# When the loads for the up-projection's sums are issued, and where the last group's second norm is worked out, in a one-core encoder layer on Trainium2

## The chip, the core and the metric

The kernel runs on one core of one Trainium2 chip, in one launch. The metric is device time in microseconds, from the start to the end of the execution. The core has TensorE (matmuls), VectorE, ScalarE and GpSimd, and SyncE, whose queue issues nearly all DMAs of this kernel, in order: a DMA that has to wait for something holds all later ones back. Each engine works through its own instructions in order, too.

## The reference

One layer of a streaming encoder, for 2048 prompt tokens and 64 sample tokens (2112 in all), in float32:

```python
mod = (c_act @ w_ada + b_ada)[:, None, :]
sh1, sc1, gt1, sh2, sc2, gt2 = jnp.split(mod, 6, -1)
h = rmsnorm(x, g1) * (1 + sc1) + sh1
proj = h @ w_in                                  # 1024 -> 512 + 4*512 + 8
u, q, k, v, o, gates = jnp.split(proj, cuts, -1)
pool_out, pool_buf_new = pool_mixer(u, pool_buf, start, w_pool, s_pool)
hs, C, n, m = mlstm_seq(q, k * HEAD_DIM ** -0.5, v, ig, lf, C, n, m)
...
mix = jnp.concatenate([pool_out, hs], -1) @ w_out
x = x + gt1 * mix
h2 = rmsnorm(x, g2) * (1 + sc2) + sh2            # the second norm
up = h2 @ w_up                                   # 1024 -> 2 * 2816
conv = b_conv + sum(w_conv[j] * upp[:, j:j + T] for j in range(CONV_W))
a, g = jnp.split(conv, 2, -1)
x = x + gt2 * ((jax.nn.silu(g) * a) @ w_down)
```

A final RMSNorm follows. The two things that the change touches are the second norm, whose factor for a token is one over the root of the mean of the squares of the token's 1024 values of x after the first half, and the up-projection's weights `w_up`.

## The kernel before, in words

All large matmuls are done in three passes of a high and a low part of each operand. Data lie with channels on partitions and tokens along the free dimension; a "row" below is 128 channels by the tokens of a group.

The **first half** (up to about 805 us of the span) goes over four groups of tokens, 512 each and 576 in the last, numbered 0 to 3. For each: the projection of v and the gates (`proj_v`, matmuls at L1091), q, k and o (`gemm`, L445), the mLSTM of each head (L1188 to L1302), the pooling mixer, and the out-projection with its residual (`outproj`), which writes the eight rows of x to the DRAM tensor `x2d` (L608). In the mLSTM of a head, VectorE copies the small gate tiles CL and GL out of PSUM and makes kw, the weighted keys; TensorE needs CL at L1201, GL at L1255 in the last group and kw at L1280. The names of the helpers stand at L237 for many of these operations.

Beside the matmuls run generators that are advanced a step at a time: `bg[0]` holds the gates and the mLSTM of the heads, `bg[1]` the norms of the next group, `bg[3]` the conditioning `ada` (VectorE steps `s<-raw,CA` and `acc<-raw,CA` at L195 and L197, whose `raw` tiles are loads of `w_ada`, L181), and `bg[4]`, from group 1 on, `up_sums`.

`up_sums` prepares the **second half**, which forms the up-projection from seven products of sums of rows and of weights instead of eight. It has 44 steps. A step loads a tile w of 128 x 1024 values of `w_up` with two DMAs (L824), makes four sums and differences of 128 x 256 in place on VectorE (L838, L839, L841, L842), and stores the tile to the DRAM tensor `wsum` (L847). There are four buffers of w, so a load into a buffer waits until the store that last read it has landed: the wait stands at the head of SyncE's queue. Three loads are issued ahead of the first step; at the end of step i the load for step i+3 is issued, and right behind it step i's own store. The sums and both kinds of DMA keep their program order among themselves; where they fall among the other instructions of VectorE and SyncE in groups 1 to 3 is decided by a scheduler that orders instructions ahead of time. From the start of the second half on, and in the first steps of group 0, TensorE, ScalarE, VectorE and GpSimd keep the written order.

The **second half** (about 805 to 2229 us) goes over three token groups of 704: up-projection (`Pair.products`, L1531, with ScalarE copies `s` and `u` at L1570 and L1579 and VectorE sums `ea` and `eg`), convolution and gate, down-projection (L1807). Its input rows hx are split into high and low parts at L738 and L745.

The **second norm** of groups 0 to 2 is worked out in the out-projection: `sq_acc` squares each finished row on ScalarE (L479, into a scratch tile) and adds it to `ssum` on VectorE (L480); then TensorE sums over the partitions and the result goes to the columns of RS2. For the last group (`o.last`) the squares and adds are the same, but the end is `stat2`: a generator on `bg[0]` that idles for twelve steps, into the first products of the second half, and then calls `rstd_cols` (TensorE, L489). The columns of RS2 of the last group are read when the input of the third token group of the second half is prepared.

Of the kernel before, what the change touches and what calls it, by code (L numbers as in the profile page):

```python
# [11 lines left out]
AF = mybir.ActivationFunctionType  # L12
ALU = mybir.AluOpType
# [5 lines left out]
KD = D // P  # L19
# [37 lines left out]
def tile_layer(ctx: ExitStack, tc: tile.TileContext, xT, vecs, cst, rst, w_mod, w_ada, w_qkou, w_v, w_pool,  # L57
               w_out, w_up, w_down, st_C, st_pool, yT, o_pool, o_C, o_m, o_conv):
    nc = tc.nc
# [34 lines left out]
    bg = ([], [], [], [], [])  # L94
# [149 lines left out]
    for g in range(NG):  # L244
        o = Grp()
# [329 lines left out]
            if k != 3:  # L575
                yield

    def stat2(o, ssum):
        out = RS2[:, 4 * o.g:4 * o.g + len(o.chunks)]
        for _ in range(12):  # L580
            yield
        rstd_cols([ssum], o, out)
        yield

    def outproj(o, mix, between):

        order = [4, 5, 6, 7, 3, 2, 1, 0]
        ssum = None if o.last else ssum_tile()
        now = Urgent(nc.vector)
        nx = [load_x(n, o) for n in (0, 1)]  # L590
        for rows in [(0, 1)] + [(n,) for n in range(2, KD)]:
            xs = nx
            Ws = [Row() for _ in rows]
            pss = [[mm_ps() for _ in o.blks] for _ in rows]
            if len(rows) == 1:
                gemm(pss[0], Ws[0], mix, o, order=order, ups=(4,))
            else:
                for W, ps in zip(Ws, pss):
                    gemm(ps, W, mix, o, ks=order[:6], order=order)
                quiet.clear()  # L600
                for W, ps in zip(Ws, pss):
                    gemm(ps, W, mix, o, ks=order[6:], order=order, late=1)
            nx = [load_x(rows[-1] + 1, o)] if rows[-1] + 1 < KD else []
            for n, x, ps in zip(rows, xs, pss):
                for (bi, pa, pb, a, b, s) in o.pieces:
                    now.scalar_tensor_tensor(out=x[:, a:b], in0=ps[bi][:, pa:pb], scalar=gt1(n, s), in1=x[:, a:b],
                                             op0=ALU.mult, op1=ALU.add)
                nc.sync.dma_start(out=x2d[n, :, o.t0:o.t0 + o.T], in_=x[:, :o.T])  # L608
            if rows[0] == 0:
                between()  # L610
                if o.last:
                    ssum = fscr("ssum")
            for n, x in zip(rows, xs):
                sq_acc(ssum, x[:, :o.T], o.T, n == 0)
        if o.last:
            bg[0].append(stat2(o, ssum))
        else:
            side.append(rstd_rows(ssum, o, RS2[:, 4 * o.g:4 * o.g + len(o.chunks)], []))

# [11 lines left out]
    def fscr(dt=F32):  # L631
        if dt in ("rb", "ssum"):
            return spare[0].tile([P, FT], F32, tag=dt, name=dt)
        return spare[0].tile([P, FT], dt, tag="fscr", name="fscr", bufs=6)
# [177 lines left out]
    if True:  # L812
# [6 lines left out]
        def up_sums():  # L819
# [12 lines left out]
            for i, (f, c) in enumerate(todo):  # L832
                w = nx.pop(0)
                yield
                yield

                a0, a1_, g0, g1 = (w[:, i, :] for i in range(4))
                pin(dve.tensor_tensor(out=g1, in0=g0, in1=g1, op=ALU.add))  # L838
                pin(dve.tensor_tensor(out=g0, in0=a0, in1=g0, op=ALU.subtract))  # L839
                yield  # L840
                pin(dve.tensor_tensor(out=a0, in0=g1, in1=a0, op=ALU.subtract))  # L841
                pin(dve.tensor_tensor(out=a1_, in0=a1_, in1=a0, op=ALU.subtract))  # L842
                yield

                if i + 3 < len(todo):
                    nx.append(load(*todo[i + 3]))
                pin(nc.sync.dma_start(out=wsum[f, :, :, c:c + 256], in_=w))  # L847

        def fold():
# [633 lines left out]
    todo = []  # L1483
# [475 lines left out]
```

## Time and profile before

| | |
|---|---|
| three runs | 2225.89, 2227.15, 2227.29 us (median 2227.15) |
| profiled execution | 2230.81 us |
| its span in the profile | 2229.0 us (1.81 us lie outside it) |
| mean granted TensorE clock | 0.996 |
| TensorE busy | 2208.9 us |
| VectorE, ScalarE, GpSimd busy | 1572.2, 1000.4, 192.5 us |
| DMA | 487.26 MB, mean 219 GB/s over the span |
| SyncE at L824, waiting for a wsum store | 100.4 us in 36 waits, longest 5.8 us |

The profile's lines name a line of the kernel, an engine and an operation, and `out<-in` by the names of the tiles, with buffer numbers left out: `w<-w_up` is a load of `up_sums`, `wsum<-w` its store. An arrow in square brackets gives the idle time of the engine ahead of the instruction, and what ended it. A wait on SyncE costs nothing by itself; it matters if a DMA behind it comes too late for an engine on which TensorE waits.

### The profile page before, as it was taken

What the parts mean: (1) busy time and instruction counts of PE and PEld (TensorE: products, weight loads), DVE (VectorE), ACT (ScalarE), POOL (GpSimd) and SP (SyncE); (2) the same over time, 40 slices, a digit from 0 to 9 for tenths busy, and PEclk for the clock granted to TensorE, in tenths of its full rate; (3) what the DMA queues carried; (4) which work ended last, traced back from release to release, by engine and by line L of the source; (5) the groups of instructions that cost most, each with busy time, mean ns of one, the idle gap of its engine ahead of it and who ended that gap; (6) DMA issues with size and microseconds to landing.
All of it is one profiled execution on the core that took longest, in us unless ns stands there. A gap on an engine that the chain in (4) does not pass through costs nothing.

```text
span 2229.0 us, 37990 instructions
## 1 busy us (share of the span) xinstructions
PE 2208.9 (99%) x13744; PEld 2102.7 (94%) x13744; DVE 1572.2 (71%) x2888; ACT 1000.4 (45%) x1981; POOL 192.5 (9%) x474
## 2 busy tenths in 40 slices
PE   8999999999999999999999999999999999999998
PEld 7888888888899999999999999999999999999998
DVE  5867668757955688687858587777766675757475
ACT  4644335234333455454536354545444343445254
POOL 0010000001000100010000210100001210101012
PEclk9999999999999999999999999999999999999999
DMA  9977997988879485747557775466458655353442
GB/s 350 330 251 228 300 305 254 306 286 266 296 253 299 148 269 164 243 163 270 179 176 243 263 263 176 156 213 198 143 160 290 196 167 167 111 171 116 145 148 81
DMA packets 284708, 487.26 MB, mean 219 GB/s; under 512 B 24640, under 2 KB 88512, under 8 KB 284520
## 3 DMA queue, kind: packets, MB, share of 16 engines
q1 hardware_dynamic: 275080, 462.52, 63.2%
q10 hardware_dynamic: 9440, 22.32, 2.6%
q8 instruction: 108, 1.77, 0.3%
q14 instruction: 80, 0.66, 0.1%
HBM read 378.68 MB, written 106.06 MB: 217 GB/s over the span
## 4 chain that ended last, share of the span: by engine, by line
PE 94%; DMA 3%; DVE 2%; issue 1%; SPq 0%; ACT 0%; POOL 0%; POOLq 0%; DVEq 0%; ACTq 0%
PE mm L1531 40%; PE mm L1807 23%; PE mm L445 23%; PE mm L1091 1%; DMA raw<-w_ada 1%; PE m L1280 1%; PE m L1300 1%; PE m L1302 1%; PE m L1265 1%; DMA wsum<-w 1%; PE mm L1028 1%; PE p L1028 1%; PE m L923 0%; PE m L1255 0%; DVE scr L237 0%
## 5 line engine op out<-in xcount | busy, mean ns | idle before, releaser
L1531 PE MATMUL mm<-hx,wt 128*128 128x352 f32 x5544 | 897.9, 323 | 1.9 <-ACT s L1570 1.3
L1531 PEld LDWEIGHTS mm<-hx,wt 128*128 128x128 f32 x5544 | 892.8, 188 | 2.6 <-ACT s L1570 1.6
L1807 PE MATMUL mm<-av,wt 128*128 128x352 f32 (+2 forms) x3168 | 514.5, 323 | 0.0
L1807 PEld LDWEIGHTS mm<-av,wt 128*128 128x128 f32 x3168 | 509.6, 188 | 1.2
L445 PE MATMUL mm<-hl,wt 128*128 128x512 f32 (+2 forms) x1920 | 389.7, 358 | 0.0
L379 ACT ACTIVATE wt<-raw 128x512 fp32r<-128x512 f32 (+3 forms) x518 | 286.2, 574 | 215.6 <-PE mm L445 77.6
L382 DVE TENSOR_TENSOR wt<-raw,wt 128x512 fp32r<-128x512 f32 (+3 forms) x518 | 324.4, 641 | 78.4 <-ACT wt L379 75.6
L445 PEld LDWEIGHTS mm<-hl,wt 128*128 128x128 f32 x1920 | 315.4, 189 | 52.5 <-issue 5.3
L1823 DVE SCALAR_TENSOR_TENSOR x<-mm,MOD,x 128x352 f32<-128x352 f32 (+4 forms) x224 | 106.5, 526 | 133.1 <-PE mm L1807 132.9
L445 PE MATMUL mm<-mx,wt 128*128 128x512 f32 (+1 forms) x960 | 185.3, 354 | 0.0
L445 PEld LDWEIGHTS mm<-mx,wt 128*128 128x128 f32 x960 | 159.1, 188 | 25.4
L1518 DVE SCALAR_TENSOR_TENSOR tg<-eg,V,tg 128x704 f32<-128x704 f32 (+1 forms) x132 | 125.7, 953 | 53.9 <-ACT tg L1513 51.6
L382 DVE TENSOR_TENSOR wt<-wt 128x512 fp32r<-128x512 f32 x176 | 121.7, 692 | 36.9 <-ACT wt L379 36.9
L1518 DVE SCALAR_TENSOR_TENSOR ta<-ea,V,ta 128x704 f32<-128x704 f32 (+1 forms) x132 | 125.7, 952 | 5.2 <-ACT ta L1513 2.6
L379 ACT ACTIVATE wt<-wt 128x512 fp32r<-128x512 f32 x176 | 108.3, 622 | 18.3 <-DMA wt<-wsum 14.6
L1579 ACT ACTIVATE u<-mm 128x352 f32<-128x352 f32 x66 | 30.7, 465 | 169.5 <-PE mm L1531 162.0
L1539 DVE TENSOR_TENSOR eg<-mm,u 128x352 f32<-128x352 f32 x154 | 70.2, 468 | 41.2 <-ACT u L1594 27.1
L1639 DVE TENSOR_TENSOR av<-tg,av 128x704 fp32r<-128x704 f32 (+1 forms) x88 | 60.6, 709 | 53.8 <-ACT av L1634 53.8
L1625 ACT ACTIVATE tg<-tg 128x704 f32<-128x704 f32 (+1 forms) x66 | 52.4, 794 | 78.5 <-DVE tg L1518 78.5
L1570 ACT ACTIVATE s<-mm 128x352 f32<-128x352 f32 x66 | 30.7, 465 | 111.4 <-PE mm L1531 106.9
L1091 PE MATMUL mm<-wt,hl 128*128 128x256 f32 (+1 forms) x576 | 70.7, 282 | 0.0
L1091 PEld LDWEIGHTS mm<-wt,hl 128*128 128x128 f32 x576 | 69.8, 188 | 0.9 <-issue 0.6
(293 smaller groups left out, 1954.3 us busy)
## 6 DMA issues: line engine op xcount, KB each, us to landing
raw<-w_up SPq DMA_DIRECT2D x198, 256.0 KB, 4.0
wt<-hl_kept SPq DMA_DIRECT2D x96, 512.0 KB, 6.0
wt<-wsum SPq DMA_DIRECT2D x176, 256.0 KB, 4.0
wt<-wsplit SPq DMA_DIRECT2D x88, 512.0 KB, 4.6
raw<-w_down SPq DMA_DIRECT2D x96, 256.0 KB, 3.0
w<-w_up SPq DMA_DIRECT2D x88, 256.0 KB, 4.0
wsum<-w SPq DMA_DIRECT2D x44, 512.0 KB, 5.1
wsplit<-wt SPq DMA_DIRECT2D x44, 512.0 KB, 3.3
```

Of the source, the lines that this page charges most:

```text
L379: act.activation(u.w[:, 0, :u.n], u.raw[:, :u.n], AF.Copy)
L382: dve.tensor_tensor(out=u.w[:, 1, :u.n], in0=u.raw[:, :u.n], in1=u.w[:, 0, :u.n].bitcast(F32), op=ALU.subtract)
L445: pe.matmul(ps[bi][:, :hi - lo], U[:, a, k % 4 * P:(k % 4 + 1) * P], mv[k][:, b, lo:hi], start=(at == 0 and pi == 0), stop=(k == order[-1] ...
L1028: pe.matmul(to[ti][:, :n], h[k][:, b, ti * P:(ti + 1) * P], w[:, a, k % 2 * n:(k % 2 + 1) * n], start=(hv == 1 and k == 0 and (a, b) == (0 ...
L1091: pe.matmul(ps[ti][:n, :cols], h[4 * kh + k4][:, b, lo:lo + n], U[:, a, k4 % 2 * cols:(k4 % 2 + 1) * cols], start=(kh == 0 and k4 == 0 and ...
L1518: dve.scalar_tensor_tensor(out=t[:, :E], in0=ext[:, j:j + E], scalar=wc(j, f), in1=t[:, :E], op0=ALU.mult, op1=ALU.add)
L1531: pe.matmul(ps[:, :FH], U[:, a, kc * P:(kc + 1) * P], Bo.at(nm, kc, b), start=(first and kc == 0 and pi == 0), stop=(kc == 3 and pi == 2), ...
L1539: dve.tensor_tensor(out=ext[:, d:d + b - a], in0=ps[:, a:b], in1=u[:, a:b], op=ALU.add)
L1625: act.activation(self.tg[:, :E], self.tg[:, :E], AF.Silu)
L1639: dve.tensor_tensor(out=self.d[:, 1, a:b], in0=self.tg[:, a + 2 * s:b + 2 * s], in1=self.d[:, 0, a:b].bitcast(F32), op=ALU.subtract)
L1807: pe.matmul(ps[i][:, :hi - lo], U[:, a, k % 4 * P:(k % 4 + 1) * P], av[k][:, b, lo:hi], start=(k == 0 and (a, b) == PASSES[0]), stop=(k == ...
L1823: dve.scalar_tensor_tensor(out=x3[n][:, a:b], in0=ps[i][:, a - lo:b - lo], scalar=gt2(n, s), in1=x3[n][:, a:b], op0=ALU.mult, op1=ALU.add)
```

## The change

In `up_sums` the load for a later step moves. Up to now it is issued at the end of step i, for step i+3, ahead of step i's store. Now it is issued in the middle of step i, ahead of the sums, for step i+2, and so behind the store of step i-1; steps 0, 42 and 43 issue none. There are still three loads ahead of the first step and four buffers.

In the out-projection of the last group, the squares and the adds are left out. `stat2` instead loads the eight rows of the group from `x2d` again (128 x 576 values, 288 KB each, SyncE), two ahead and then one per step, into scratch tiles of the second half; it squares them on ScalarE and adds them on VectorE, a step of the generator for each, and then calls `rstd_cols` as before. It runs during the first products of the second half.

```diff
-    def stat2(o, ssum):
-        out = RS2[:, 4 * o.g:4 * o.g + len(o.chunks)]
-        for _ in range(12):
-            yield
-        rstd_cols([ssum], o, out)
+    def stat2(o):
+
+        def load(k):
+            x = fscr()
+            nc.sync.dma_start(out=x[:, :o.T], in_=x2d[k, :, o.t0:o.t0 + o.T])
+            return x
+        nx = [load(0), load(1)]
+        ssum = fscr("ssum")
+        yield
+        for k in range(KD):
+            x = nx.pop(0)
+            yield
+            act.activation((x if k else ssum)[:, :o.T], x[:, :o.T], AF.Square)
+            yield
+            if k:
+                dve.tensor_tensor(out=ssum[:, :o.T], in0=ssum[:, :o.T], in1=x[:, :o.T], op=ALU.add)
+            if k + 2 < KD:
+                nx.append(load(k + 2))
+        yield
+        rstd_cols([ssum], o, RS2[:, 4 * o.g:4 * o.g + len(o.chunks)])
         yield
...
             if rows[0] == 0:
                 between()
-                if o.last:
-                    ssum = fscr("ssum")
             for n, x in zip(rows, xs):
-                sq_acc(ssum, x[:, :o.T], o.T, n == 0)
+                if not o.last:
+                    sq_acc(ssum, x[:, :o.T], o.T, n == 0)
         if o.last:
-            bg[0].append(stat2(o, ssum))
+            bg[0].append(stat2(o))
...
                 w = nx.pop(0)
                 yield
                 yield
+                if 0 < i < len(todo) - 2:
+                    nx.append(load(*todo[i + 2]))
 
                 a0, a1_, g0, g1 = (w[:, i, :] for i in range(4))
...
                 yield
-
-                if i + 3 < len(todo):
-                    nx.append(load(*todo[i + 3]))
                 pin(nc.sync.dma_start(out=wsum[f, :, :, c:c + 256], in_=w))
```

The line numbers of the kernel after the change are larger: by 15 in the lines from `outproj` on (L608 is L623), by 14 or 13 from `up_sums` on (L824 is L838, L847 is L860, L1280 is L1293, L1531 is L1544).

## The prediction

> **What bounds the kernel now.** I read the page's engine busy times and chain first, then the waits of TensorE, then the windows by stage, then the timeline around each wait that the change can reach.
>
> ```profile
> PE 2208.9 (99%) x13744; PEld 2102.7 (94%) x13744; DVE 1572.2 (71%) x2888; ACT 1000.4 (45%) x1981; POOL 192.5 (9%) x474
> PE 94%; DMA 3%; DVE 2%; issue 1%; SPq 0%; ACT 0%; POOL 0%; POOLq 0%; DVEq 0%; ACTq 0%
> ```
> ```profile
> PE m L1255 <- DVE GL L237: 2.0, 1, 2.0
> PE m L1280 <- DVE kw L237: 2.0, 1, 2.0
> PE mm L1531 <- ACT s L1570: 1.3, 1, 1.3
> PE mm L1531 <- DVE hx L745: 0.6, 1, 0.6
> ```
> ```profile
> 218.00:270.00 52.00, 50.04 (x324) 44.45 (x324) 33.45 (x67) 13.67 (x28) 1.01 (x1) 0.97 0.91 301
> 440.00:576.00 136.00, 136.00 (x678) 110.44 (x677) 96.60 (x217) 58.08 (x147) 10.51 (x16) 1.00 0.85 276
> 576.00:645.00 69.00, 67.00 (x501) 63.59 (x500) 49.38 (x102) 19.87 (x47) 1.11 (x1) 1.00 0.86 288
> 801.00:830.00 29.00, 27.15 (x175) 26.54 (x174) 22.24 (x46) 14.16 (x28) 2.90 (x6) 1.00 0.76 245
> ```
> TensorE is busy 99% of the span, and the change neither adds nor removes a matmul: it can only win back stalls or make new ones. VectorE (71%) and ScalarE (45%) are not the bound over a stage, so the work on them that moves costs only where TensorE waits behind it. In the windows (columns: length, busy TensorE, weight loads, VectorE, ScalarE, GpSimd, then granted clock, DMA share, GB/s) TensorE is idle 1.96, 2.00 and 1.85 us in the three stages where such waits stand, and not at all in 440 to 576. The reach of the change is therefore a few microseconds out of 2229, around 0.3%. I call the stalls A (266), B (642) and C (807 and 811).
>
> **Stall A, group 1.** The chain of waits, then the timeline:
>
> ```profile
> 252.82 3.92 DMA wsum<-w
> 256.75 0.55 SPq L824
> 258.30 0.56 SPq L847
> 258.92 5.12 DMA raw<-w_ada
> ```
> ```profile
> 264.13 0.75 DVE L197 SCALAR_TENSOR_TENSOR s<-raw,CA,s 128x512 f32<-128x512 f32 x1 [7.70 <-DMA raw<-w_ada]
> 265.54 0.69 DVE L237 TENSOR_TENSOR kw<-m,CL 128x512 f32<-128x512 f32 x1
> 266.38 1.82 PE L1280 MATMUL m<-va,kw 128*128 128x129 f32 x8 [1.96 <-DVE kw L237]
> 267.84 4.03 PE L445 MATMUL mm<-hl,wt 128*128 128x512 f32 x12
> ```
> Read it from the bottom: TensorE waits for kw; kw is queued on VectorE behind a conditioning step (s, acc) that idled 7.70 us for its w_ada load; SyncE could issue that load only at 258.92, because the w_up load ahead of it stood until a store to wsum had landed (252.82 + 3.92). The wait is 1.96 us, and then come slow matmuls: 8 in 1.82 us and 12 in 4.03 us. The same forms in group 2 are below.
>
> ```profile
> 435.64 3.89 PE L445 MATMUL mm<-hl,wt 128*128 128x512 f32 x16
> 437.09 0.56 SPq L847 DMA_DIRECT2D wsum<-w  x1
> 448.34 0.69 DVE L237 TENSOR_TENSOR kw<-m,CL 128x512 f32<-128x512 f32 x1 [3.06 <-PE m L1255]
> 449.67 1.05 PE L1280 MATMUL m<-va,kw 128*128 128x129 f32 x8
> ```
> There 8 take 1.05 us and 16 take 3.89 us (243 ns each, against 336). The slow stretch costs 0.77 + 12 x 0.093 = 1.9 us more, and A costs 3.9 us in all. The granted clock confirms it:
>
> ```profile
> 266.40:270.00 3.60, 3.60 (x13) 3.21 (x14) 3.21 (x9) 0.00 (x0) 0.00 (x0) 0.53 1.04 333
> 642.80:647.00 4.20, 4.20 (x32) 4.01 (x33) 3.76 (x10) 0.00 (x0) 0.00 (x0) 1.00 0.68 239
> ```
> It is 0.53 after A and 1.00 after B, whose wait was as long. So a new wait of some 2 us costs 2 or 4 us, and I can't tell which.
>
> [...]
>
> After the change, in the built order: SyncE issues two wsum stores back to back, a kept-weights load, then the w_up load (again until the first store lands, so again about 256.75), one more kept-weights load of 512 KB, the third store, then w_ada. VectorE still has s and acc ahead of kw; only GL moved ahead of them. So w_ada leaves at 258.92 + 0.35 at the earliest and has up to 512 KB more ahead of it; at the 301 GB/s of this window that is 1.7 us. Stall A doesn't go; it grows by 0.3 to 2.0 us, **I take +1.2**. Far ends: -3.9 if the load lands 2 us sooner after all, and +2.
>
> **Stall B, group 3.**
>
> ```profile
> 629.85 1.20 SPq L824 DMA_DIRECT2D w<-w_up  x2
> 631.74 0.26 DVE L237 COPY CL<-m 128x16 f32<-128x16 f32 x2 [5.72 <-PE m L1188]
> 631.95 0.49 ACT L237 ACTIVATE CL<-m 128x16 f32<-128x16 f32 x6 [0.37 <-DVE CL L237]
> 635.82 1.20 SPq L824 DMA_DIRECT2D w<-w_up  x2
> 636.50 0.60 PE L1201 MATMUL m<-CL,C 128*128 128x16 f32 x4
> 640.82 0.42 DVE L838 TENSOR_TENSOR w<-w 128x256 f32<-128x256 f32 x1 [6.68 <-DMA w<-w_up]
> 642.77 0.30 PE L1255 MATMUL m<-V,k 128*64 128x128 f32 x1 [2.00 <-DVE GL L237]
> ```
> GL stood behind four w sums (640.82 on, 0.42 us each), whose load left at 635.82. In the built order after, the sums ahead of GL are of a tile loaded long before, and GL is done around 639.3, ahead of the need at 640.8: the 2.00 us go. But another tile's four sums now stand ahead of the CL copies. Their load waits for a wsum store as the one at 629.85 did; its second half is issued 0.6 us later, at 630.45, and with the 3.8 us that such loads take here (row below) it lands at about 634.3. Four sums end at 636.0, CL (0.26) and its ScalarE part (0.49) at 636.8, hand-overs aside, against the need at 636.50. A new wait of 0 to 2 us, **I take 0.5**; B nets **-1.5** (-2.0 to 0).
>
> ```profile
> w<-w_up SPq DMA_DIRECT2D x6, 256.0 KB, 3.8
> ```
>
> **Group 2, where there is no wait now.** kw is done at 449.03 and needed at 449.67, a slack of 0.6 us. In the built order after, kw stands behind conditioning steps of two w_ada loads and one w sum, and those loads stand on SyncE behind a w_up load that waits for a wsum store to land: the pattern of A, in a second place. The store follows sums that end where the present one's do, so it leaves at about 437.1 and lands 3.8 us later (rows below, from 432 to 452), at 440.9; two w_up loads and a kept-weights load take SyncE 1.9 us; the two w_ada loads leave at 442.8 and 443.4 and land at about 448.0 and 448.6. Ahead of kw then remain two steps of s and acc and a sum (0.75 x 3 + 0.42 us), so kw ends near 451.1: **+1.4 us**. Low end 0 (loads 1.4 us earlier), high end 4 (the price of A with its slow clock).
>
> ```profile
> wsum<-w SPq DMA_DIRECT2D x3, 512.0 KB, 3.8
> raw<-w_ada SPq DMA_DIRECT2D x2, 256.0 KB, 5.2
> ```
>
> **Stall C, start of the second half.**
>
> ```profile
> 807.37 2.52 PE L1531 MATMUL mm<-hx,wt 128*128 128x352 f32 x14 [0.59 <-DVE hx L745]
> 809.69 0.69 ACT L479 ACTIVATE scr<-scr 128x576 f32<-128x576 f32 x1 [0.96 <-DVE scr L237]
> 810.82 0.76 DVE L480 TENSOR_TENSOR ssum<-ssum,scr 128x576 f32<-128x576 f32 x1
> 811.16 5.09 PE L1531 MATMUL mm<-hx,wt 128*128 128x352 f32 x30 [1.26 <-ACT s L1570]
> 813.39 0.52 DVE L1583 TENSOR_TENSOR ea<-mm,s 128x352 f32<-128x352 f32 x1
> ```
> The last out-projection's squares (0.69 us on ScalarE) and adds (0.75 us on VectorE) sit among the first products' splits and copies: the hx wait is behind an earlier add, the s wait behind the last square. Both leave this spot, and in the built order nothing takes their place ahead of hx and s: -1.85 us. Eight squares and seven adds come back between the products' copies, with eight loads of 288 KB. The cost there: the third product's ea (now 813.39, 1.85 us sooner without the waits) is queued behind the first add, which needs a reload issued at about 804.3 and a square; with the 5.3 us of the row below the load lands at 809.6, square and add end at 811.2 if they start at once, about 1 us later behind other copies, and TensorE needs ea at about 813. A wait of 0 to 1.5 us, **I take 0.35**; C nets **-1.5** (-1.85 to 0). The remaining seven steps have 1 to 4 us of slack each, VectorE and ScalarE being 77% and 49% busy in 801 to 830; without that cover they would cost 15 x 0.7 = 10 us. The sum's own matmuls (10, moved 36 matmuls later) gate nothing before the third token group.
>
> ```profile
> x<-x2d SPq DMA_DIRECT2D x7, 352.0 KB, 5.3
> ```
> The reloads add 2.36 MB; at the 245 GB/s of that stage 9.6 us of transfer spread over some 20 us, with the DMA share at 0.76.
>
> **The sum**, against the profiled execution (span 2229.0, 2230.81 with what lies around it): A +1.2, B -1.5, group 2 +1.4, C -1.5, together **-0.4**. That execution lies 3.66 us above the median of 2227.15; I apply the difference to the median: **2226.7 us**. Part of those 3.66 may be stall A's slow clock, which other executions need not have.
>
> **Rivals.** (0.2% is 4.5 us, about what a measurement of this kernel can tell from no change.)
> 1. *All three stalls go and none comes.* If the w_ada loads land 2 us sooner than I count, A goes too and group 2 keeps its slack: -3.9 - 2.0 - 1.85 = -7.8, or 2219.4; with A's clock alone kept, near -5.8. For it: loads now leave as soon as stores land. Against it: in the built order kw still stands behind w_ada, and w_ada behind the same store. Chance 0.13.
> 2. *Slower: the wait for kw takes two places.* Place: VectorE's kw in group 2, behind w_ada. Price: 2 us and 1.9 us of slow clock, as at A; A grows by its 2.0, B and C give back 1.0 each: 2.0 + 1.9 + 2.0 - 2.0 = +3.9, up to +6 if CL adds its 2: 2231 to 2233. It decides from the point at which the two w_ada loads land later than about 448.6. [...] Against: three of four terms must fall badly. Chance 0.17.
> 3. *The reload path costs in the second half* (ea, or weights whose issue is 4 us later on SyncE): +1.5 on C, 2228.2; it stays within 0.2%, and is part of the same case.
>
> **How the numbers follow.** Forecast with rival 3: 0.70, from 2222.9 to 2231.5. Faster by over 0.2%: 0.13 (rival 1). Slower by over 0.2%: 0.17 (the upper part of rival 2 and what I haven't seen). Low ends: B -2.0, C -1.85, A and group 2 at 0 give -3.85, and 1 us more for part of A's clock makes 2222.3; the high end is +4.4, in the middle of rival 2: 2231.5.
>
> **What would show it.** In the profile after: the wait of L1293 (now L1280) for kw still near 266 and 2 to 4 us long; a second one near 450; no wait for GL; at most 1.5 us for a CL matmul near 637; no wait for hx and s near 807 to 811. I am wrong if w_ada lands before 263 in group 1, if group 2 has no wait, or if waits for ea, weights or rows appear after 812.

## The result, and the profile after

| | before | after |
|---|---|---|
| median of 4 runs | 2227.22 us | 2240.5 us (2238.15 to 2242.28) |
| ratio, 95% interval | | 1.0058 [1.0045, 1.0071] |
| profiled execution, its span | 2230.81, 2229.0 us | 2241.95, 2240.2 us |

The changed kernel is 13.3 us (0.58%) slower. The forecast was 0.4 us faster; the result lies outside its range and on the side that had a chance of 0.17. Beside other kernels it was measured again, and lay 7.8 us above the kernel before (1.0040 [1.0027, 1.0053]); both intervals are clear of no change.

I read the views in the order of the prediction. The page first: busy times, the chain that ended last by engine.

```profile
PE 2211.4 (99%) x13744; PEld 2104.9 (94%) x13744; DVE 1570.8 (70%) x2888; ACT 1000.5 (45%) x1981; POOL 195.9 (9%) x474
PE 92%; DMA 4%; DVE 2%; issue 1%; SPq 1%; ACT 0%; POOL 0%; POOLq 0%; DVEq 0%; ACTq 0%
```
The matmuls are the same 13744; TensorE's share of the chain fell from 94% to 92%, and DMA's rose from 3% to 4%. The averages say no more than that. The waits of TensorE (total us, times, longest):

```profile
PE m L1293 <- DVE kw L237: 5.6, 2, 3.2
PE mm L445 <- ACT k L1222: 3.6, 1, 3.6
PE mm L1544 <- ACT wt L379: 2.2, 1, 2.2
```
The waits for GL, hx and s are gone. There are two for kw in place of one, and two that did not exist: for a k (L1222) and for a weight tile (L379). The windows place them (columns as in the prediction):

```profile
218.00:270.00 52.00, 48.85 (x315) 43.31 (x314) 33.05 (x68) 13.64 (x28) 1.01 (x1) 0.97 0.93 316
440.00:576.00 136.00, 133.13 (x655) 107.25 (x654) 97.47 (x216) 55.25 (x142) 10.95 (x16) 0.99 0.81 273
645.00:742.00 97.00, 93.42 (x659) 86.83 (x658) 48.73 (x137) 33.66 (x108) 5.39 (x8) 0.95 0.79 251
801.00:830.00 29.00, 29.00 (x202) 28.97 (x201) 24.13 (x52) 15.38 (x31) 0.00 (x0) 1.00 0.83 262
```
Idle TensorE: 3.15 us in group 1, 2.87 in group 2, none where B and C were (576 to 645, where B was, is busy throughout), and 3.58 us at a granted clock of 0.95 in 645 to 742, a stretch that was fully busy before:

```profile
645.00:742.00 97.00, 97.00 (x719) 90.56 (x718) 55.53 (x157) 39.25 (x130) 9.23 (x15) 1.00 0.75 245
```

**Where the time came from.** TensorE runs nearly the same order in both kernels, so the start of the same matmul in both traces, counted from each span's start, is a running account. The first and the last matmul of three lines, before and then after ("first and last start us"):

```profile
L1255 PE MATMUL m<-V,k x37: 270/273/330, 262.2 to 642.8; 128*128 128x128 f32 x36, 128*64 128x128 f32 x1
L1280 PE MATMUL m<-va,kw x104: 271/275/426, 266.4 to 730.4; 128*128 128x129 f32 x96, 64*128 64x129 f32 x8
L1531 PE MATMUL mm<-hx,wt x320: 317/323/429, 805.0 to 860.0; 128*128 128x352 f32 x160
```
```profile
L1268 PE MATMUL m<-V,k x37: 272/273/330, 260.6 to 645.5; 128*128 128x128 f32 x36, 128*64 128x128 f32 x1
L1293 PE MATMUL m<-va,kw x104: 271/275/554, 266.0 to 741.2; 128*128 128x129 f32 x96, 64*128 64x129 f32 x8
L1544 PE MATMUL mm<-hx,wt x249: 318/323/427, 815.8 to 859.9; 128*128 128x352 f32 x125
```
(The last pair's counts differ because that view was cut off at 860 us; only its first start is used.)

| point | before | after | after minus before | step |
|---|---|---|---|---|
| first L1255 / L1268, ahead of A | 262.2 | 260.6 | -1.6 | -1.6, start-up |
| first kw matmul (A) | 266.4 | 266.0 | -0.4 | +1.2 |
| kw matmul of group 2 | 449.67 | 452.81 | +3.1 | +3.5 |
| last L1255 / L1268, behind B | 642.8 | 645.5 | +2.7 | -0.4 |
| last kw matmul, behind group 3's heads | 730.4 | 741.2 | +10.8 | +8.1 |
| first product of the second half | 805.0 | 815.8 | +10.8 | 0 |
| end of the span | 2229.0 | 2240.2 | +11.2 | +0.4 |

The start-up's -1.6 arises in the first 60 us, where the order is the same in both kernels: it differs from run to run (the granted clock there is 0.94 before, 1.00 after, and 0.97 in the repeat e6). The largest step, +8.1 us, is one place in group 3, which I call D. I take the places in order.

**A, group 1.** The chain of after, in order of time (start, duration):

```profile
250.80 3.29 DMA wsum<-w
254.10 0.60 SPq L838
...
257.47 6.28 DMA raw<-w_ada
...
264.51 0.74 DVE acc L197
265.26 0.61 DVE kw L237
```
The chain of before, still: a store lands, the w_up load leaves (L838 is the old L824), then w_ada, then s, acc and kw. With start-up's lead of 1.6 us taken out, w_ada leaves 0.15 us later, and takes 6.28 us where it took 5.12.

**Group 2.** The timeline of after:

```profile
440.52 1.25 SPq L838 DMA_DIRECT2D w<-w_up  x2
442.48 1.37 SPq L181 DMA_DIRECT2D raw<-w_ada  x2
446.08 1.64 PE L445 MATMUL mm<-hl,wt 128*128 128x512 f32 x6 [0.39 <-DMA wt<-hl_kept]
449.65 0.75 DVE L197 SCALAR_TENSOR_TENSOR s<-raw,CA,s 128x512 f32<-128x512 f32 x1 [3.94 <-DMA raw<-w_ada]
451.98 0.68 DVE L237 TENSOR_TENSOR kw<-m,CL 128x512 f32<-128x512 f32 x1
452.81 1.34 PE L1293 MATMUL m<-va,kw 128*128 128x129 f32 x8 [2.48 <-DVE kw L237]
```
kw stands behind s and acc, which wait on VectorE for a w_ada load: issued at 442.48, used at 449.65, 7.2 us. TensorE waits 2.48 us, after another 0.39 for a kept weight tile. The w_up load ahead of w_ada on SyncE (440.52) waits for no store: SyncE's waits between 434 and 450 hold none for wsum.

**D, group 3.** The chain of after:

```profile
681.78 7.35 DMA wsum<-w
...
689.75 3.64 DMA w<-w_up
...
693.83 1.12 DVE nd L237 x4
...
698.77 0.51 DVE mx L712
699.30 0.59 ACT mx L714
699.89 0.28 ACT k L1222
```
and the timeline of after at that place, then of before at the same work:

```profile
679.22 1.20 SPq L838 DMA_DIRECT2D w<-w_up  x2
682.40 0.65 SPq L724 DMA_DIRECT2D mx<-x2d  x1
689.56 0.58 DVE L712 SCALAR_TENSOR_TENSOR mx<-mx,G,mx 128x352 f32<-128x352 f32 x1 [6.50 <-DMA mx<-x2d]
690.97 0.35 DVE L237 SCALAR_TENSOR_TENSOR nd<-m,CL,nd 128x129 f32<-128x129 f32 x1
693.49 0.42 DVE L854 TENSOR_TENSOR w<-w 128x256 f32<-128x256 f32 x1 [2.16 <-DMA w<-w_up]
700.22 3.10 PE L445 MATMUL mm<-hl,wt 128*128 128x256 f32 x11 [3.58 <-ACT k L1222]
```
```profile
673.40 0.65 SPq L710 DMA_DIRECT2D mx<-x2d  x1
680.30 1.08 DVE L698 SCALAR_TENSOR_TENSOR mx<-mx,G,mx 128x352 f32<-128x352 f32 x2
682.34 1.23 DVE L237 SCALAR_TENSOR_TENSOR nd<-m,CL,nd 128x129 f32<-128x129 f32 x4 [0.29 <-ACT nd L237]
683.57 0.41 DVE L838 TENSOR_TENSOR w<-w 128x256 f32<-128x256 f32 x1
```
Read the chain from the top. A wsum store takes 7.35 us. The w_up load into its buffer stands at the head of SyncE's queue until then and lands at 693.4. On VectorE a sum of that tile (L854) waits for it, and behind the sum stand the nd steps that finish a head of the mLSTM; behind those come an mx step, the scaling of mx on ScalarE, and, behind that on ScalarE, the copy of k that empties a PSUM bank. TensorE stops for the bank (3.58 us). Before, nd (682.34) ran ahead of the sum (683.57), whose tile was there. The links span two engines and one DMA queue; only the last is a wait of TensorE.

The chain shows only what came last. VectorE had already stood 6.50 us for rows mx, read back from x2d (689.56), ahead of the first nd step (690.97). The read left at 682.40, behind a w_up load (679.22) that had itself waited 4.0 us for a store; before, it left at 673.40, ahead of the next w_up load (679.36), and mx (680.30) waited for nothing. So two steps came late ahead of the nd steps: the rows mx and a sum. How much each counts is read from the experiments (e5 and e9).

**Second half.** The timeline of after:

```profile
830.99 0.63 ACT L379 ACTIVATE wt<-wt 128x512 fp32r<-128x512 f32 x1 [2.96 <-DMA wt<-wsum]
833.57 3.14 PE L1544 MATMUL mm<-hx,wt 128*128 128x352 f32 x18 [2.17 <-ACT wt L379]
```
A weight tile read back from wsum comes 2.17 us late, among the loads of x2d; that takes the place of the waits for hx and s (1.85 us).

### The profile page after: what moved, and what is told of

It is laid out like the page before. It is cut to its first block, busy times and chain, and to the rows that moved or that the text cites. A ratio compares the mean times of both kernels' runs of the same rounds, so it can differ in the third digit from the quotient of the medians.

```text
span 2240.2 us, 38003 instructions
## 1 busy us (share of the span) xinstructions
PE 2211.4 (99%) x13744; PEld 2104.9 (94%) x13744; DVE 1570.8 (70%) x2888; ACT 1000.5 (45%) x1981; POOL 195.9 (9%) x474
## 4 chain that ended last, share of the span: by engine, by line
PE 92%; DMA 4%; DVE 2%; issue 1%; SPq 1%; ACT 0%; POOL 0%; POOLq 0%; DVEq 0%; ACTq 0%
PE mm L1544 39%; PE mm L445 23%; PE mm L1820 23%; PE mm L1104 2%; DMA raw<-w_ada 2%; PE m L1293 1%; DMA mx<-w_mod 1%; PE m L1315 1%; PE m L1313 1%; PE m L1278 1%; DMA raw<-w_qkou 1%; DMA wsum<-w 0%; PE m L1268 0%; DMA k<-w_mod 0%; PE m L873 0%
## 5 line engine op out<-in xcount | busy, mean ns | idle before, releaser
L1544 PE MATMUL mm<-hx,wt 128*128 128x352 f32 x5544 | 897.5, 323 | 2.2 <-ACT wt L379 2.2
L1544 PEld LDWEIGHTS mm<-hx,wt 128*128 128x128 f32 x5544 | 892.8, 188 | 2.5 <-ACT wt L379 2.4
L445 PE MATMUL mm<-hl,wt 128*128 128x512 f32 (+2 forms) x1920 | 394.9, 361 | 4.0 <-ACT k L1222 3.6
L379 ACT ACTIVATE wt<-raw 128x512 fp32r<-128x512 f32 (+3 forms) x518 | 286.5, 574 | 221.8 <-PE mm L445 83.8
L1531 DVE SCALAR_TENSOR_TENSOR tg<-eg,V,tg 128x704 f32<-128x704 f32 (+1 forms) x132 | 125.7, 952 | 53.1 <-ACT tg L1526 50.7
L1531 DVE SCALAR_TENSOR_TENSOR ta<-ea,V,ta 128x704 f32<-128x704 f32 (+1 forms) x132 | 125.6, 952 | 5.1 <-ACT ta L1526 2.7
L379 ACT ACTIVATE wt<-wt 128x512 fp32r<-128x512 f32 x176 | 108.7, 623 | 32.9 <-DMA wt<-wsum 28.0
L1104 PE MATMUL mm<-wt,hl 128*128 128x256 f32 (+1 forms) x576 | 70.7, 282 | 0.0
L1104 PEld LDWEIGHTS mm<-wt,hl 128*128 128x128 f32 x576 | 69.8, 188 | 0.9 <-issue 0.6
```

The costliest lines, as they stand in the source:

```text
L379: act.activation(u.w[:, 0, :u.n], u.raw[:, :u.n], AF.Copy)
L445: pe.matmul(ps[bi][:, :hi - lo], U[:, a, k % 4 * P:(k % 4 + 1) * P], mv[k][:, b, lo:hi], start=(at == 0 and pi == 0), stop=(k == order[-1] ...
L1104: pe.matmul(ps[ti][:n, :cols], h[4 * kh + k4][:, b, lo:lo + n], U[:, a, k4 % 2 * cols:(k4 % 2 + 1) * cols], start=(kh == 0 and k4 == 0 and ...
L1531: dve.scalar_tensor_tensor(out=t[:, :E], in0=ext[:, j:j + E], scalar=wc(j, f), in1=t[:, :E], op0=ALU.mult, op1=ALU.add)
L1544: pe.matmul(ps[:, :FH], U[:, a, kc * P:(kc + 1) * P], Bo.at(nm, kc, b), start=(first and kc == 0 and pi == 0), stop=(kc == 3 and pi == 2), ...
```

## The experiments

The theory that I formed from this: the mid-step loads alone carry the loss. The order on VectorE and SyncE is fixed before the kernel runs; the move of one load per step changes which steps that wait for a DMA (the conditioning's s and acc, the sums of w_up, the rows mx) stand ahead of steps of the mLSTM that TensorE needs (kw, GL, nd, at), and one late landing holds back the steps behind it (in group 2, kw behind an s step that waited 3.94 us). Its rivals: the second norm's reload carries it; or the w_ada loads are late only because SyncE, their queue, is blocked by waits for stores; or the store landings are the one cause, and a further buffer cures it.

All kernels were timed in five rounds beside the kernel before:

| kernel | us | before beside it | ratio [95%] |
|---|---|---|---|
| e1 mid-step loads alone | 2237.62 | 2229.07 | 1.0036 [1.0023, 1.0049] |
| e2 second norm alone | 2228.2 | 2229.07 | 0.9998 [0.9989, 1.0006] |
| e3 after, w_ada on GpSimd's queue | 2243.38 | 2229.07 | 1.0061 [1.0047, 1.0075] |
| e4 before, w_ada on GpSimd's queue | 2244.14 | 2229.07 | 1.0066 [1.0053, 1.0078] |
| e5 after, five buffers | 2235.73 | 2229.41 | 1.0036 [1.0025, 1.0048] |
| e6 after, repeated | 2237.24 | 2229.41 | 1.0040 [1.0027, 1.0053] |
| e7 before, five buffers | 2235.14 | 2229.41 | 1.0024 [1.0013, 1.0035] |
| e8 after, w_ada a step earlier | 2235.59 | 2229.41 | 1.0032 [1.0020, 1.0043] |
| e9 after, conditioning later | 2240.72 | 2229.15 | 1.0056 [1.0043, 1.0069] |
| e10 before, conditioning later | 2231.91 | 2229.15 | 1.0018 [1.0009, 1.0027] |
| e11 second norm, conditioning later | 2234.21 | 2229.15 | 1.0019 [1.0006, 1.0032] |
| e12 as e11, norm later too | 2236.02 | 2229.15 | 1.0033 [1.0020, 1.0046] |
| e13 five buffers, four ahead | 2237.59 | 2228.11 | 1.0051 [1.0037, 1.0065] |
| e14 as e13, conditioning later | 2238.11 | 2228.11 | 1.0050 [1.0038, 1.0063] |
| e15 five buffers, conditioning later | 2233.96 | 2228.11 | 1.0028 [1.0018, 1.0039] |

Idle TensorE by stage, from the windows of each profile (us):

| window | before | after | e6 | e1 | e2 | e5 | e7 | e8 | e9 | e15 |
|---|---|---|---|---|---|---|---|---|---|---|
| 218:275 (A) | 1.96 | 3.15 | 2.14 | 1.98 | 0.63 | 3.48 | 0.31 | 2.40 | 0 | 0 |
| 440:480 (group 2) | 0 | 2.87 | 2.48 | 2.27 | 0 | 3.55 | 0.79 | 1.33 | 3.03 | 0 |
| 576:645 (B) | 2.00 | 0 | 0 | 0 | 1.60 | 0 | 0 | 0.39 | 0 | 0 |
| 645:742 (D) | 0 | 3.58 | 3.25 | 4.21 | 0.13 | 1.64 | 5.08 | 3.76 | 5.30 | 4.17 |
| 801:840 (C) | 1.85 | 2.48 | 1.25 | 2.28 | 1.45 | 2.01 | 1.66 | 2.23 | 1.08 | 1.57 |

### Which of the two edits: e1 and e2

e1 takes the sums' edit alone:

```diff
+                if 0 < i < len(todo) - 2:
+                    nx.append(load(*todo[i + 2]))
...
-                if i + 3 < len(todo):
-                    nx.append(load(*todo[i + 3]))
```


> The mid-step loads alone; the second norm of the last group stays in the out-projection. Its order on every engine is that of the changed kernel up to the end of the first half, and that of the kernel before from there on. Theory (the stalls belong to the two edits separately): the new waits for kw at about 264 and 450 and the new wait for the copy of k at about 697 are all there, GL's wait is gone, and the waits for hx and s at the start of the second half are back. From the first-half ledger of the changed kernel (+1.2, +0.75, +4.3, -2.05, +7.8) this is 12 us over the kernel before: 2239, give or take 3 for clock terms. Rival (the long wait at 697 comes from the second-norm edit, through rows and scratch tiles that come free at other times): without that edit the wait at 697 is gone, and the kernel is 4 us over the kernel before, 2231.

e2 takes the other alone (of its edit, only the call is shown here):

```diff
-            bg[0].append(stat2(o, ssum))
+            bg[0].append(stat2(o))
```


> The second norm of the last group alone, worked out in the second half from rows in DRAM; loads of the sums as before. Theory: first half as before (kw 2 us at 266, GL 2 us at 642), the waits for hx and s gone (-2.0), a late weight tile (about +2.2) and the sum over partitions with its wait (about +0.5 beyond its own matmuls) in their place: +0.7, 2228, so not to be told from no change. Rival (the edits act together): 7 to 8 us slower, 2235, with a wait at about 697.

e1 is 8.55 us slower, e2 0.9 us faster, which its interval does not tell from nothing. The waits of e1:

```profile
PE m L1279 <- DVE kw L237: 4.2, 2, 2.3
PE mm L445 <- ACT k L1208: 2.7, 1, 2.7
```
Both waits for kw and the wait for k at D come with the sums' edit alone. In e2 the waits for hx and s are gone, and one of its own is there:

```profile
PE mm L1545 <- DVE eg L1553: 1.4, 1, 1.4
```
That eg is queued behind the fifth of the seven adds of the reloaded squares, which had itself waited 4.17 us for its square; the prediction had put such a wait at the third product's ea, behind the first add. So the second norm's edit makes no difference that its interval can tell, and the loss is the loads'.

### Is w_ada blocked on SyncE: e3 and e4

The w_ada loads go to GpSimd's queue, in the changed kernel (e3) and in the kernel before (e4):

```diff
-                nc.sync.dma_start(out=got[i], in_=src[i])
+                nc.gpsimd.dma_start(out=got[i], in_=src[i])
```


> The changed kernel with the w_ada loads of groups 1 to 3 issued from GpSimd's queue instead of SyncE's, so that they no longer stand behind up-projection loads that wait for a store to land. Theory (kw is late because w_ada is queued behind such a load): both waits for kw go, with their slow clock, some 5 and 4 us: 2231 or so, the wait at 697 staying. Rival (w_ada is late because the DMA engines are full, in whatever queue it stands): the waits for kw stay within 1 us, 2240.

> The kernel before with the same move of the w_ada loads. Theory: the one wait for kw at 266 goes, with its slow clock: 2223. Rival (full DMA engines): 2227, the wait at 266 as before.

No wait for kw is left in either. That fits w_ada as what held kw, but the order is built anew around the loads, so it doesn't show it. In e3, TensorE waits 6.3 us for va at L1104 instead (two waits, the longest 4.1): the conditioning steps now stand ahead of the gates in the projection of v. At 1.0061 and 1.0066 of the kernel before, both are as slow as the changed kernel (1.0058 and 1.0040). The expectation on the total missed, and the two kernels do not tell whether SyncE's queue was the cause.

### Is it the stores' landing: e5, e6, e7

e5 gives the sums five buffers, so that a load waits for a store that is a step older (one nd buffer makes room, and the two other places that use these buffers get the same `bufs`); e7 does the same to the kernel before; e6 is the changed kernel again, as a base.

```diff
-                w = a1.tile([P, 4, 256], F32, tag="w4", name="w4", bufs=4)
+                w = a1.tile([P, 4, 256], F32, tag="w4", name="w4", bufs=5)
...
-            nd = a2.tile([P, 5, 129], F32, tag="nd", name="nd")
+            nd = a2.tile([P, 5, 129], F32, tag="nd", name="nd", bufs=1)
```


> The changed kernel with five buffers for the tiles of the sums, so that a load no longer waits for the store of the step two before it (room is made by one nd buffer instead of two, which by itself changes no order). The order of TensorE and GpSimd is the same, that of VectorE, ScalarE and SyncE differs in a few places. Theory (SyncE stands at the head of its queue until a store has landed, and what is behind it comes late): the w_ada loads of group 2 leave 1 to 2 us earlier and the wait for kw there falls from 2.5 to about 1 us with no slow clock; the w_up load ahead of nd at 693 leaves 3 us earlier and the wait at 697 falls to about 1 us with no slow clock: some 8 us less than the changed kernel, 2232. Rival (the order of VectorE alone does it, or the full DMA engines): the waits stay within 1 us, 2240.

> The changed kernel as it is, beside the other kernels of this comparison. Expected 13 us over the kernel before, with the waits for kw at 264 and 450 (2 to 4 us each) and the wait for the copy of k at about 697 (3 to 4 us); how far the waits and the slow clock behind them differ between executions is read from it.

> The kernel before with the same five buffers. Theory: the w_ada load of group 1 no longer stands behind a w_up load that waits for a store, so the wait for kw at 266 falls by 1 to 2 us; the load behind the sums ahead of GL leaves earlier too: 3 to 5 us less than the kernel before, 2223, unless the order that the scheduler makes of it puts a late load elsewhere. Rival: no change, 2227.

In e5 the wait for k at D is gone (1.64 us idle in 645 to 742, clock 1.00), and those for kw have grown:

```profile
PE m L1293 <- DVE kw L237: 7.0, 2, 3.5
```
But that does not single out the stores' landing. SyncE still waits for them at D, 3.9 and 2.1 us at the two w_up loads there, against 4.0 and 3.1 in the changed kernel. What is gone is the lateness on VectorE: in this order no sum stands ahead of the nd steps, and the rows mx come sooner. The idle time of VectorE ahead of the nd steps, for rows and for the sum's tile, against TensorE's wait for k (us):

| | rows mx | sum's tile | both | wait for k | difference |
|---|---|---|---|---|---|
| changed kernel | 6.50 | 2.16 | 8.66 | 3.58 | 5.08 |
| e6, repeated | 5.50 | 2.83 | 8.33 | 3.25 | 5.08 |
| e1, loads alone | 6.06 | 1.72 | 7.78 | 2.69 | 5.09 |
| e8, w_ada earlier | 7.16 | 1.66 | 8.82 | 3.76 | 5.06 |
| e9, conditioning later | 7.64 | none ahead | 7.64 | 2.17 | 5.47 |
| e5, five buffers | 1.08 | none ahead | 1.08 | none | |

In the first four, TensorE waits for what the two make together, less 5.1 us: so long can VectorE stand here before TensorE waits, and that is the slack of this place. In e9 the rows alone are enough:

```profile
685.62 0.59 DVE L712 SCALAR_TENSOR_TENSOR mx<-mx,G,mx 128x352 f32<-128x352 f32 x1 [7.64 <-DMA mx<-x2d]
693.72 3.36 PE L445 MATMUL mm<-hl,wt 128*128 128x256 f32 x12 [2.17 <-ACT k L1222]
```
So D is mostly the late rows, and the sum's tile adds to them. A store's landing is a link in that chain, ahead of the w_up load that the rows stand behind; that it is what makes the rows late isn't shown.

In group 2 of e5 the w_ada loads leave at 441.47, 0.2 us ahead of the s step before (441.65), and the next s, which needs them, starts at 449.58: 8.1 us. In e6 they leave at 440.07, 0.45 us ahead of that step (440.52), and s starts at 446.52: 6.4 us. In both, as in the changed kernel, no wait for a store stood ahead of it there; what is late is its landing. The DMA share in 440 to 480, 0.89 and 0.95, does not explain that: it was 0.91 before, where such loads took 5.2 us. The waits of SyncE itself point the wrong way: the change took those at this load (L824, now L838) from 100.4 to 54.0 us, and the kernel got slower.

In e7 the wait for kw at A is gone (0.31 us idle there, for at), and GL no longer waits; but the order at A is another one, with kw ahead of the conditioning step. A wait of 0.8 us for kw comes in group 2, and 5.08 us of idle TensorE in 645 to 742, where the kernel before had none; the longest wait there, 3.8 us, is for at (L1280). That missed what I expected of the total: a further buffer doesn't help the kernel before either.

### Earlier or later conditioning: e8 to e12

e8 issues the w_ada loads four steps ahead instead of three:

```diff
-        lead = 4 if first else 3
+        lead = 4
```


> The changed kernel with the w_ada loads issued four steps of the conditioning ahead instead of three. In the built order kw in group 2 stands behind one such load instead of two. Theory (kw is late only through the w_ada load ahead of it): the wait for kw in group 2 falls by the second step of s and acc and the later landing, about 1.5 to 2.5 us, and its slow clock may go; the wait at 697 stays: 2236 to 2238. Rival (the sums and stores bunched behind the gates are what counts): no change, 2240.

The waits for kw fall from 4.3 (e6) to 3.7 us, group 2's idle time from 2.48 to 1.33; the wait for k at D is 3.8 us (3.2). Against e6 the total gains 1.6 us, which the intervals don't tell from nothing.

e9 (changed kernel) and e10 (kernel before) start the conditioning of groups 1 to 3 behind the first head's projections, so that kw of the first head stands ahead of it:

```diff
-            if o.g > 0:
-                bg[3].append(ada(2 + o.g, False))
...
+                if hd == 0 and o.g > 0:
+                    bg[3].append(ada(2 + o.g, False))
```


> The changed kernel, in which groups 1 to 3 start the conditioning after the projections of the first head instead of ahead of the projection of v. In the built order no step of it stands ahead of the first head's kw any more in groups 1 and 2; the mid-step loads and the second norm are as changed. Theory (kw is late because it is queued on VectorE behind a step whose w_ada load lands 6 to 8 us after it is issued, so what counts is that step's place and the bytes queued ahead of its load): both waits for kw go, with their slow clock (4 to 9 us by the profiles of the changed kernel); the wait for the copy of k at about 697 stays: 2231 to 2234. Rival (sums of the up-projection, bunched behind the gates, hold kw back whatever else stands there): waits for kw of 2 us each stay, 2238.

> The kernel before with the same later start of the conditioning. One step still stands ahead of kw in group 1, but its load is issued earlier in the queue. Theory: the wait for kw at 266 (0.6 to 2 us, with up to 1.9 us of slow clock) shrinks or goes, the wait for GL stays: 2 us less than the kernel before, at most 4. Rival: steps moved into the later heads meet late loads there, no gain or a loss.

In both, A is gone: 218 to 275 is fully busy. In group 2 of e9, kw waits behind the sums of a late w_up tile instead:

```profile
447.25 0.42 DVE L854 TENSOR_TENSOR w<-w 128x256 f32<-128x256 f32 x1 [5.13 <-DMA w<-w_up]
448.88 2.06 PE L1293 MATMUL m<-va,kw 128*128 128x129 f32 x8 [2.99 <-DVE kw L237]
```
The total hardly moved (1.0056 against 1.0058 and 1.0040), which is not what I expected, and 5.30 us stand idle in 645 to 742. e10 loses A as well, gets 2.7 us of waits for the state st, and waits 2.5 for GL (2.0 before). It is slower than the kernel before, as its rival had it.

e11 is e2 with the same diff; e12 also starts the second norm eight steps later and its sum over the partitions six:

```diff
-            if o.g > 0:
-                bg[3].append(ada(2 + o.g, False))
...
+                if hd == 0 and o.g > 0:
+                    bg[3].append(ada(2 + o.g, False))
```


> The second norm in the second half, the loads of the sums as before, and the conditioning started later. Theory (the parts add up): the norm alone was 0.9 us under the kernel before, within its interval; with the wait for kw gone 2 to 4 us less than the kernel before, 2225 to 2227 where that has 2229. Rival: as the kernel before.

```diff
+        for _ in range(8):
+            yield
         nx = [load(0), load(1)]
...
-        yield
+        for _ in range(6):
+            yield
         rstd_cols([ssum], o, RS2[:, 4 * o.g:4 * o.g + len(o.chunks)])
```


> As the one before it, but the second norm waits eight steps before its first loads and six more before its sum over the partitions, so that its adds and loads do not stand ahead of the third product's eg and its matmuls do not wait for the last add. Theory (the 1.4 us wait for eg and the 0.5 us wait for the last add are what ate the gain of the norm edit): 1.5 to 2 us less than the one before it. Rival (some product's copies stand behind the adds wherever these are): the same as the one before it.

Both have new waits for st (3.7 and 4.4 us); the later norm has 1.5 us for ea. These were attempts at a version faster than both kernels, and they failed: both expected a gain.

### Both causes at once: e13 to e15

e13 has five buffers and four loads ahead of the first step, so that the mid-step load is for step i+3:

```diff
-            nx = [load(*todo[i]) for i in range(3)]
+            nx = [load(*todo[i]) for i in range(4)]
...
-                if 0 < i < len(todo) - 2:
-                    nx.append(load(*todo[i + 2]))
+                if 0 < i < len(todo) - 3:
+                    nx.append(load(*todo[i + 3]))
```


> The changed kernel with five buffers (one nd buffer), and the load in mid-step for step i+3 instead of i+2, four loads ahead of the first step: a load still waits only for the store of two steps before, but has one more step of time until its sums. In the built order two w_ada steps still stand ahead of kw in group 1 and two in group 2. Theory A (a load's late landing, whichever load stands ahead of the mLSTM's operations on VectorE, is what TensorE waits for): the waits for kw stay at 2 us or more, each, because w_ada is no earlier, and the long wait of the first half's last group (697) goes, since sums find their data: 2233 to 2236. Theory B (sums' loads are the only late ones): all three go, 2228.

e14 adds the later conditioning to e13, and e15 adds it to e5:

```diff
-            if o.g > 0:
-                bg[3].append(ada(2 + o.g, False))
...
+                if hd == 0 and o.g > 0:
+                    bg[3].append(ada(2 + o.g, False))
```


> The same with the conditioning of groups 1 to 3 started after the first head's projections. What stands ahead of the first head's kw, GL and CL are then sums whose loads were issued a step earlier. Theory A: no wait over 1 us for kw, GL or the copy of k is left in groups 1 and 2 and at 697: 2226 to 2228, at the kernel before or under it by up to 3. Theory C (as in the last comparison: what is taken away from one place turns up ahead of another of the mLSTM's operations, because the order is made with earlier landings than the chip gives): a wait of 2 to 4 us at another place, 2233 or more.

> The changed kernel with five buffers and the later conditioning, loads for step i+2 as changed. Theory A: between the two before it and the changed kernel, since in group 2 sums whose load was issued only two steps before stand ahead of GL and kw: a wait of 1 to 2 us there, 2231 to 2234. Theory C: 2235 or more, with waits at new places.

In e13 the wait for k is gone as in e5, and one of 3.7 us for an mx tile (L213 behind L471) is there instead; kw waits 4.0 us. e14 has 3.6 us for kw in three places and 2.2 for st. So more time for the sums' loads is no cure: e13 is slower than I expected (2237.59 against 2233 to 2236), and e14 has waits at other places, as its theory C had it. In e15 nothing is left to wait for in groups 1 and 2 (218 to 576 is fully busy at a clock of 1.00), where I had expected 1 to 2 us. The sums of a late tile still stand ahead of GL and kw in group 2, and wait, but in time:

```profile
443.82 0.42 DVE L854 TENSOR_TENSOR w<-w 128x256 f32<-128x256 f32 x1 [3.33 <-DMA w<-w_up]
```
The last group keeps 4.17 us idle (1.8 for at, 2.3 for st), at a clock of 0.98, and the kernel is still 0.28% slower than before. That late landings ahead of kw make the waits of A is shown: moving the conditioning alone takes A away, in e9 and e10. In group 2 it is supported by e9 and e15; e14, with the loads a step earlier still, keeps up to 1.7 us there. At D the table above shows it for the wait for k. But group 3 has further steps in line, and each version with mid-step loads keeps some other wait there.

## Why the prediction was wrong, point by point

- **A, +1.2.** Right in its chain: w_ada behind the same store, leaving a little later and taking longer; e9 and e10 show that the place of the conditioning decides. That the account has just +1.2 is partly luck: with the same order at A, the wait is 3.15 us in the profiled execution, 2.14 in e6 and 1.98 in e1, and in e2, with the order of before, it is 0.63 where before had 1.96. One execution differs from another by as much as the term.
- **B, -1.5.** Right in kind: the wait for GL is gone, the new one for CL didn't come. From the kw matmul of group 2 to the end of B the account moves by -0.4: the 2.0 us won, and by difference 1.6 us for the slow matmuls behind group 2's wait (of which 1.3 by an estimate, the missing share of the granted clock times the busy time, (1 - 0.88) x 11.13 us in 445 to 459).
- **Group 2, +1.4.** The place was right, the size wrong: +3.5 at the kw matmul (2.48 of wait, 0.39 for a weight tile, the rest in small steps) and +1.6 of slow clock. The loads left when I said, 442.48 against 442.8, but not for the reason that I gave: the w_up load ahead of them did not stand for a store, so that part of the pattern of A wasn't there, and the time fitted by luck. The mis-sized term is the 5.2 us from issue to landing, a median over 432 to 452 of before; here it was 7.2 us, in e6 6.4, in e5 8.1. The point from which rival 2 decides (landing later than 448.6) was passed.
- **C, -1.5.** The gain came (hx and s no longer wait; 801 to 830 fully busy) and was eaten by rival 3, at +2.2 for a late weight tile in place of +1.5. From the first product to the end: +0.4. I had written that waits for weights after 812 would show me wrong, and they did. The slack of 1 to 4 us that I gave the later steps was too much: the fifth add stood 4.55 us for its square here, and 4.17 in e2, where it held eg. e2 puts the whole edit at no change.
- **Rival 2** had the right side. Its second place is there in e1 too, where A itself did not grow (1.98 us idle). Its price, 3.9 to 6 us with what B and C give back, fits the account without start-up and D: +1.2 + 3.5 - 0.4 + 0.4 = +4.7. The time that it named, 2231 to 2233, was missed because of D.
- **D, not in the sum: +8.1.** This is the step that failed. I checked the built order around each wait of the profile and in group 2, and left out 645 to 742 because TensorE was fully busy there, which put its change at nothing without a reason. A stage without a wait only has slack, here 5.1 us, and the change moves loads and sums in all three groups: VectorE stood 6.50 and 2.16 us for the rows mx and a sum's tile, ahead of nd. 3.58 us are TensorE's wait; the rest is mostly the slow clock behind it, 0.77 over 694 to 716, by the same estimate (1 - 0.77) x 18.42 = 4.2 us. The step comes again: in e6 the same two matmuls lie 95.3 us apart against 87.6 before, +7.7. e1 shows that it comes with the sums' edit, e9 that the late rows alone are enough for a wait, and e5 that the wait for k is gone with both late steps.
- **The clock.** I couldn't tell whether a wait of 2 us costs 2 or 4, and left the clock out of the middle of the forecast. In the profiled execution A, group 2 and D all lost clock. In e6 A and group 2 did not, and D did. e6's span is 5.8 us shorter (2234.4), and most of that is accounted for: 1.2 us ((1 - 0.83) x 6.85) and 1.3 of slow clock, both by that estimate, 1.3 less wait for kw, 0.4 less for k, 1.0 less in the second half (1.2 for eg in place of 2.2), together 5.2. That the distance between +13.3 and +7.8 in the medians is of this kind is argued from these two profiles, and no run isolates it.

The sums of the prediction hold, but for one bound: its low end of 2222.9 is not the 2222.3 that its terms make. Nothing hangs on it.

What stays open: why the scheduler puts which step where, since every edit gave another order; and group 3, where each version with mid-step loads kept 1.6 to 5.3 us of idle TensorE. Nor do the profiles account for all of e15: its span is 2230.6 us against 2229.0, while the medians are 5.9 us apart. The spans of all runs agree with the medians: 2231.8 us in the middle for e15, 2226.3 for the kernel before beside it. So the profiled execution of the kernel before is a long one. It lies 3.7 us above its median and holds A's slow clock and the 0.94 of the start; e2, with the same order at A, had 0.63 us idle there and no slow clock, so executions of one kernel differ by about as much.

## What to carry to other kernels

If the order of an engine's instructions is fixed ahead of time, look in the built order for each step that waits for a DMA ahead of a step on the path, in the stages too where the profile shows no wait now, and set its lateness against the slack there (5.1 us at D). Price such a place with a range of landing times (6.4 to 8.1 us in group 2 here), not with the median of the kernel before (5.2), and add the slow clock that may follow (by the estimate above 4.2 us at D; nothing at A and in group 2 of e6). Shorter waits at the head of a queue are no gain by themselves: SyncE's waits fell from 100.4 to 54.0 us, and the kernel lost 8 to 13 us.

## What the runs showed of the hardware

Like waits were followed by different clocks. The windows behind A, group 2 and D in the changed kernel, then in its repeat:

```profile
262.00:272.00 10.00, 6.85 (x32) 5.72 (x31) 7.18 (x15) 0.00 (x0) 0.00 (x0) 0.83 0.79 294
445.00:459.00 14.00, 11.13 (x53) 8.54 (x53) 8.96 (x21) 1.74 (x5) 0.82 (x1) 0.88 0.89 327
694.00:716.00 22.00, 18.42 (x102) 16.76 (x102) 13.11 (x38) 8.03 (x25) 1.72 (x2) 0.77 0.84 272
```
```profile
262.00:272.00 10.00, 7.86 (x49) 6.64 (x48) 8.88 (x23) 1.92 (x10) 0.00 (x0) 1.00 0.84 306
445.00:459.00 14.00, 11.82 (x69) 9.85 (x69) 12.17 (x30) 5.16 (x20) 0.24 (x1) 1.00 0.93 334
694.00:716.00 22.00, 20.75 (x120) 18.86 (x121) 11.52 (x31) 9.19 (x30) 0.00 (x0) 0.77 0.87 273
```
Waits of 3.15, 2.48 and 3.58 us were each followed by a lower clock (0.83, 0.88 and 0.77 in these windows); in the repeat, waits of 2.14 at A and 2.18 in group 2 were not (1.00), and one of 3.25 at D was (0.77). In e1 2.7 us at D left the clock at 1.00, while in the kernel before 1.96 us at A were followed by 0.53 (266.40 to 270.00). So the length of the wait alone doesn't tell which of these lost clock; what does isn't shown. Behind the wait at D of the changed kernel, with a clock of 0.50, 12 matmuls of one form took 3.36 us (700.22), and 1.85 us once it was back at 1.00 (711.76).
